# One feed-forward chunk and a copy of the first input chunk at another distance from the weights

## The chip, the cores and the metric

One NeuronCore of a Trainium2 chip runs the whole kernel; the other cores are idle. The metric is the device time of one execution in microseconds (us). TensorE (PE, with its weight loads as PEld), VectorE (DVE), ScalarE (ACT), GpSimd (POOL) and SyncE (SP) each work through a queue of their own, in order, and wait for one another by semaphores.

## The reference: what is computed

Two layers (`DEPTH = 2`) over 256 tokens of width 1024. Each layer is a half-step SwiGLU feed-forward (FFN), a token mixer with three attention branches, and a second feed-forward, each inside a sandwich of RMS norms and with shift, scale and gate from a conditioning vector. The part that the change touches:

```
def swiglu(h, w_gate, w_up, w_down):
    return (jax.nn.silu(h @ w_gate) * (h @ w_up)) @ w_down

for l in range(DEPTH):
    h = modulate(x, norm_pre[l, 0], ...);  x = residual_add(x, swiglu(h, ...), ...)
    h = modulate(x, norm_pre[l, 1], ...);  x = residual_add(x, token_mixer(h, ...), ...)
    h = modulate(x, norm_pre[l, 2], ...);  x = residual_add(x, swiglu(h, ...), ...)
```

`w_gate` and `w_up` are 1024 x 2816, `w_down` is 2816 x 1024, so there are four feed-forwards in a run. They are called FFN0 to FFN3 here, in order of time: FFN0 and FFN1 are those of layer 0, FFN2 and FFN3 those of layer 1.

## The kernel before, in words

Activations lie transposed in SBUF: 128 partitions are 128 of the features, and 256 columns are the tokens. Every fp32 operand of a product is split into a high part of type `float32r` and a low remainder, and a product is three matmuls (`mm3`, L172 to L174): high weights by high activations, high weights by low activations, low weights by high activations. The weights are the loaded (stationary) operand, 128 x 128, and the activations stream past them, 128 x 256. `lin` runs `mm3` over the 128-row chunks k of the contraction into one PSUM tile, so a gate or up tile takes 8 x 3 = 24 matmuls, and a down tile 22 x 3 = 66. Each matmul comes with a weight load of its own.

The modulated input of a feed-forward is `hT[0][k]` and `hT[1][k]` (tiles `h0`, `h1`, high and low, k = 0 to 7; `hact(i, k)` picks one). The inner activation is `mid[0][n]` and `mid[1][n]`, n = 0 to 21, each a tile of 256 columns or 1024 bytes per partition. Weights arrive by SP's DMA queue as `raw`, ACT casts them to `whi` (L166) and DVE subtracts to `wlo` (L167), six buffers each. Small pads (`gap`, 64 bytes or some more) stand between the allocations. By the allocation of the built program every chunk of `h` and `mid` that is streamed begins at a byte address that is 288 modulo 512, and every 128-column weight tile that is loaded beside it at 352 modulo 512; the distance from weights to activations is thus -64 bytes (modulo 512) for nearly all of the kernel's matmuls.

`ffn` (from L353) has these stages. Three of the four feed-forwards begin with an entry: `enter` starts the first six gate tiles from the raw residual (L279, 258 columns, streamed from the tiles `wd8_*`, whose rows are 1032 bytes apart), then `finish` makes the eight modulated chunks (`pn` on DVE L249, `h0` on ACT L251, `h1` on DVE L252), and PE runs the first three up tiles side by side as the chunks appear. FFN0 begins with `opening` instead, which does eight gate and eight up tiles chunk by chunk as the weights arrive. Then comes the loop over `todo`, one `lin` per gate or up tile: 28 tiles in FFN0 and 38 in each other one (the first three of the 38 are those that run side by side). `evac` empties a tile: a SiLU on ACT for gate tiles, and for up tiles a product on DVE (`m`, L379), a cast on ACT to `mid[0][n]` (L383) and a subtraction on DVE to `mid[1][n]` (L384). The last stage is the down projection: four groups of two output tiles, chunk 0 to 21, 132 matmuls each.

The order on each engine is set by the tile framework: it takes the instructions in program order, except that those under `high_priority` come earlier and those under `issue_after` behind a named one, and it estimates when an engine is free. So a new instruction can move others beside it.

Of the kernel before, what the change touches and what calls it, by code (L numbers as in the profile page):

```python
# [11 lines left out]
F32 = mybir.dt.float32  # L12
F32R = mybir.dt.float32r
# [6 lines left out]
S = 256  # L20
DFF = 2816
KC = D // 128
EPS = 1e-6
NEG = -1e30
NO = 8
GATED = 0.65


@with_exitstack
def trunk(ctx, tc, x, c, vecs, ada_w, w_gate, w_up, w_down, w_in, w_uq, w_ukv, w_branch, w_out, rope, out):  # L30
    nc = tc.nc
# [76 lines left out]
    for i in range(0, D, 512):  # L108
        p = ps(512)
# [66 lines left out]
    def lin(o, w, wk, cols, act, ak, nk, start, stop):  # L176

        for k in range(nk):
            mm3(o, w(0, wk + k, cols), w(1, wk + k, cols), act(0, ak + k), act(1, ak + k),
                start and k == 0, stop and k == nk - 1)  # L180
# [45 lines left out]
    def gap(pool, nbytes, name):  # L226
        pool.tile([128, nbytes // 4], F32, name=name)
# [123 lines left out]
    NF = DFF // 128  # L351

    def ffn(l, f, s, opening=None, ahead=None):  # L353
        with ExitStack() as es:
            midp = es.enter_context(tc.tile_pool(name="mid", bufs=1))
            ftmp = es.enter_context(tc.tile_pool(name="ftmp", bufs=2))
            if opening is None:
                wdp = es.enter_context(tc.tile_pool(name="wdp", bufs=1))
                gap(wdp, 64, "gap4")
            mid = [[midp.tile([128, S], F32R, name=f"mid{i}_{n}") for n in range(NF)] for i in range(2)]  # L360
            sg = {}
            last_silu = [None]

# [34 lines left out]
            if opening is None:  # L398
                todo = ([(0, n) for n in range(6)] + [(1, n) for n in range(6)] + todo[12:])
                first = [(ps(S + 2, kind="lin" if i < 2 else "att"),) + weights(*t) for i, t in enumerate(todo[:6])]  # L400
                rp, finish = enter(l, s, first, [wdp.tile([128, FIRST], F32R, name=f"wd8_{i}") for i in range(2)])
                evac(*todo[0], first[0][0], rp)
                finish()
                for i in range(1, 6):
                    evac(*todo[i], first[i][0], rp)
                todo = todo[6:]
            else:
                opening(W, evac)
            for i, (src, n) in enumerate(todo):
                ada_until(l, s, GATED * i / len(todo))  # L410
                p = ps()
                w, cols = weights(src, n)
                lin(p, w, 0, cols, hact, 0, KC, True, True)
                evac(src, n, p)
            table_after(SQRT, last_silu[0])
            if opening is not None:
# [2 lines left out]
            gc = post_col(l, s, 0.5)  # L419
            if opening is not None:  # L420
                wdp = es.enter_context(tc.tile_pool(name="wdp", bufs=1))
                gap(wdp, 64, "gap4")
            for g in range(D // 256):
                pp = [ps(), ps()]
                for k0 in range(0, NF, 8):
# [575 lines left out]
```

## Time and profile before

| | us |
|---|---|
| median of 3 runs | 1311.8 |
| lowest, highest run | 1305.99, 1315.94 |
| the profiled execution, whole | 1306.87 |
| its span, first to last instruction | 1305.0 |
| PE busy in the span | 1279.3 (98%) |
| DVE busy | 990.3 (76%) |
| ACT busy | 758.6 (58%) |

The profile is of one execution. "Busy" for PE counts the time in which at least one matmul is under way; matmuls overlap one another (one lasts 0.28 us, and the next begins about 0.12 us after it), so a busy PE can still be faster or slower. What counts is the time from one matmul's start to the next one's, here called the pitch. Times in the rows are us from the span's start.

### The profile page before, as it was taken

The numbers are of one execution on the slowest core, as the hardware profiler recorded it, in microseconds if no ns is written. First come the engines' busy times: TensorE is split into PE (matmuls) and PEld (weight loads), VectorE is DVE, ScalarE is ACT, GpSimd is POOL, SyncE is SP. The second block draws the span as 40 slices with busy tenths as digits, with TensorE's granted clock in tenths as the row PEclk, the third lists the DMA queues.
The fourth block names the chain that finished last, engine by engine and source line by source line (L and its number), as shares of the span: only waits on it lengthen the run. The fifth ranks groups of instructions, "written<-read, shape, count | busy, mean of one in ns | idle before, by whom it ended". The sixth has DMA issues, their size and how long they took to land.

```text
span 1305.0 us, 26411 instructions
## 1 busy us (share of the span) xinstructions
PE 1279.3 (98%) x10626; PEld 1236.9 (95%) x10626; DVE 990.3 (76%) x1717; ACT 758.6 (58%) x1284; POOL 70.5 (5%) x140
## 2 busy tenths in 40 slices
PE   7999999999999999999999999999999999999997
PEld 6999999998899999999999999999898999999997
DVE  8987777768778798777698777786767969976552
ACT  4655555665865665554565554477577665745551
POOL 0000100000000000001000001000000000000000
PEclk9999999999999999999999999999999999999999
DMA  9988782636567647888928888645467477585550
GB/s 358 364 303 301 272 313 99 195 118 219 199 234 249 213 167 260 268 273 282 322 82 289 277 265 297 243 138 175 149 214 247 163 246 249 155 284 185 177 186 33
DMA packets 82924, 295.73 MB, mean 227 GB/s; under 512 B 9201, under 2 KB 9585, under 8 KB 82802
## 3 DMA queue, kind: packets, MB, share of 16 engines
q1 hardware_dynamic: 64370, 226.94, 50.7%
q0 software_dynamic: 18432, 67.12, 15.8%
q8 instruction: 83, 1.36, 0.4%
q14 instruction: 39, 0.32, 0.1%
HBM read 292.97 MB, written 1.05 MB: 225 GB/s over the span
## 4 chain that ended last, share of the span: by engine, by line
PE 91%; ACT 4%; DVE 3%; issue 1%; DMA 0%; SPq 0%
PE lin L172 25%; PE lin L174 25%; PE lin L173 24%; PE att L279 5%; PE lin L279 3%; PE att L865 1%; PE sum L547 1%; PE lin L865 1%; ACT whi L166 1%; DVE wlo L167 1%; PE att L582 1%; PE att L557 1%; DVE h L252 1%; PE att L611 1%; PE sum L194 1%
## 5 line engine op out<-in xcount | busy, mean ns | idle before, releaser
L167 DVE TENSOR_TENSOR wlo<-raw,whi 128x1024 fp32r<-128x1024 f32 (+2 forms) x382 | 453.0, 1197 | 145.5 <-ACT whi L166 140.2
L172 PE MATMUL lin<-h,whi 128*128 128x256 f32 x1808 | 503.2, 281 | 1.3 <-DVE m L379 1.0
L173 PE MATMUL lin<-h,whi 128*128 128x256 f32 x1808 | 501.7, 279 | 2.2 <-DVE h L252 2.0
L166 ACT CAST whi<-raw 128x1024 fp32r<-128x1024 f32 (+2 forms) x382 | 391.9, 1033 | 189.1 <-PE lin L173 147.3
L174 PE MATMUL lin<-h,wlo 128*128 128x256 f32 x1808 | 501.0, 278 | 0.4 <-DVE wlo L167 0.4
L172 PEld LDWEIGHTS lin<-h,whi 128*128 128x128 f32 x1808 | 338.7, 188 | 5.5 <-ACT h L251 2.6
L173 PEld LDWEIGHTS lin<-h,whi 128*128 128x128 f32 x1808 | 339.7, 188 | 3.8 <-DVE h L252 3.8
L174 PEld LDWEIGHTS lin<-h,wlo 128*128 128x128 f32 x1808 | 338.9, 188 | 0.9 <-DVE wlo L167 0.9
L119 DVE SCALAR_TENSOR_TENSOR ada<-ada,cb 128x1024 f32<-128x1024 f32 x128 | 153.9, 1219 | 25.7 <-DMA ada<-in_ada_w_dram 25.7
L172 PE MATMUL lin<-mid,whi 128*128 128x256 f32 x592 | 164.9, 278 | 0.0
L173 PE MATMUL lin<-mid,whi 128*128 128x256 f32 x592 | 164.9, 278 | 0.0
L174 PE MATMUL lin<-mid,wlo 128*128 128x256 f32 x592 | 164.9, 278 | 0.0
L133 POOL DMA_DIRECT2D ada<-in_ada_w_dram x128 | 67.7, 529 | 1048.1 <-DVE ada L119 1024.5
L173 PEld LDWEIGHTS lin<-mid,whi 128*128 128x128 f32 x592 | 111.8, 189 | 0.0
L172 PEld LDWEIGHTS lin<-mid,whi 128*128 128x128 f32 x592 | 111.8, 189 | 0.0
L174 PEld LDWEIGHTS lin<-mid,wlo 128*128 128x128 f32 x592 | 111.1, 188 | 0.0
L383 ACT CAST mid<-m 128x256 fp32r<-128x256 f32 x88 | 35.1, 407 | 74.6 <-DVE m L379 74.6
L172 PE MATMUL lin<-ybhi,whi 128*128 128x256 f32 x192 | 54.3, 283 | 2.0 <-DVE gb L536 2.0
L173 PE MATMUL lin<-yblo,whi 128*128 128x256 f32 x192 | 53.6, 279 | 0.0
L174 PE MATMUL lin<-ybhi,wlo 128*128 128x256 f32 x192 | 53.6, 279 | 0.0
L384 DVE TENSOR_TENSOR mid<-m,mid 128x256 fp32r<-128x256 f32 x88 | 36.5, 421 | 14.7 <-ACT mid L383 14.7
L370 ACT ACTIVATE sg<-lin 128x256 f32<-128x256 f32 x65 | 24.5, 380 | 31.2 <-PE lin L174 31.2
(288 smaller groups left out, 1912.8 us busy)
## 6 DMA issues: line engine op xcount, KB each, us to landing
ada<-in_ada_w_dram POOLq DMA_DIRECT2D x128, 512.0 KB, 5.0
raw<-in_mix_w_in_dram SPq DMA_DIRECT2D x100, 512.0 KB, 5.1
raw<-in_ffn_w_gate_dram SPq DMA_DIRECT2D x88, 512.0 KB, 5.1
raw<-in_ffn_w_up_dram SPq DMA_DIRECT2D x88, 512.0 KB, 5.4
raw<-in_ffn_w_down_dram SPq DMA_DIRECT2D x80, 512.0 KB, 4.8
raw<-in_mix_w_branch_dram SPq DMA_DIRECT2D x24, 512.0 KB, 5.6
oada<-in_ada_w_dram SPq DMA_DIRECT2D x16, 512.0 KB, 7.3
raw<-in_mix_w_out_dram SPq DMA_DIRECT2D x16, 512.0 KB, 5.3
```

The costliest lines, as they stand in the source:

```text
L119: return nc.vector.scalar_tensor_tensor(raw, raw, 1.0, cb, op0=OP.mult, op1=OP.mult, accum_out=modc[:, l, i, k:k + 1])
L133: nc.gpsimd.dma_start(raw, ada_w[al, i * D + k * 128:i * D + k * 128 + 128, :])
L166: nc.scalar.copy(hi, raw)
L167: nc.vector.tensor_sub(lo, raw, hi.bitcast(F32))
L172: nc.tensor.matmul(o, whi, ahi, start=start, stop=False)
L173: nc.tensor.matmul(o, whi, alo, start=False, stop=False)
L174: nc.tensor.matmul(o, wlo, ahi, start=False, stop=stop)
L279: done.append(nc.tensor.matmul(p[:, cols_of], w(i, k, cols), act[j][:, cols_of], start=start and i == j == 0, stop=stop and j == 1, skip_g ...
L370: last_silu[0] = nc.scalar.activation(sg[n], p[:, :S], AF.Silu)
L383: nc.scalar.copy(mid[0][n], m)
L384: anchor[:] = [nc.vector.tensor_sub(mid[1][n], m, mid[0][n].bitcast(F32))]
L865: nc.tensor.matmul(banks[j][:, a * 256:(a + 1) * 256], parts[k][a][i == 1][:, j * 128:(j + 1) * 128], hact(i == 2, k), start=(k == 0 and a ...
```

## The change

Three things change, all in `ffn`. The tiles of the last inner chunk, `mid[0][21]` and `mid[1][21]`, become longer (by 128 and by 16 columns), and the chunk is a view that begins 126 and 14 columns, that is 504 and 56 bytes, into its tile. The pad `gap4` (64 bytes) goes away, so that what follows lies 576 - 64 = 512 bytes further on than before. And a copy of the first modulated chunk, `hT[i][0]`, is made in that view by one cast on ACT and one on DVE; the tiles at positions 2, 4 and 9 of `todo` stream the copy as their chunk k = 0. The view is overwritten with the inner chunk 21 later. The values that are computed are the same.

```
--- before.py
+++ after.py
@@ -23,6 +23,7 @@
 NO = 8
+TURNS = (2, 4, 9)
 GATED = 0.65
@@ -356,8 +357,13 @@
             if opening is None:
                 wdp = es.enter_context(tc.tile_pool(name="wdp", bufs=1))
-                gap(wdp, 64, "gap4")
-            mid = [[midp.tile([128, S], F32R, name=f"mid{i}_{n}") for n in range(NF)] for i in range(2)]
+            mid = [[midp.tile([128, S + (0 if n < NF - 1 else (128, 16)[i])], F32R, name=f"mid{i}_{n}")
+                    for n in range(NF)] for i in range(2)]
+
+
+            for i, at in enumerate((126, 14)):
+                mid[i][-1] = mid[i][-1][:, at:at + S]
+            turned = lambda i, k: mid[i][-1] if k == 0 else hT[i][k]
             sg = {}
             last_silu = [None]
@@ -406,11 +412,13 @@
                 todo = todo[6:]
             else:
                 opening(W, evac)
+            nc.scalar.copy(mid[0][-1], hT[0][0].bitcast(F32))
+            nc.vector.tensor_copy(mid[1][-1], hT[1][0].bitcast(F32))
             for i, (src, n) in enumerate(todo):
                 ada_until(l, s, GATED * i / len(todo))
                 p = ps()
                 w, cols = weights(src, n)
-                lin(p, w, 0, cols, hact, 0, KC, True, True)
+                lin(p, w, 0, cols, turned if i in TURNS else hact, 0, KC, True, True)
                 evac(src, n, p)
             table_after(SQRT, last_silu[0])
             if opening is not None:
@@ -419,7 +427,6 @@
             gc = post_col(l, s, 0.5)
             if opening is not None:
                 wdp = es.enter_context(tc.tile_pool(name="wdp", bufs=1))
-                gap(wdp, 64, "gap4")
```

By the allocation of the built program only chunk 21 changes its address modulo 512: its high part begins at 280 (-72 bytes from the weights, was -64) and its low part at 344 (-8 bytes from the weights, was -64). All else that a matmul reads keeps its distance. The instructions that stream the shifted view are 3 x 3 in each gate and up stage and 8 x 3 in each down projection, 33 per feed-forward and 132 in all.

The first place is PE's queue in FFN0, at the third tile of `todo`. In the names, `lin_889` or `lin_891` is the tile before it, `h0`, `h1` are the modulated chunks and `mid0_21`, `mid1_21` the shifted view. Before:

```order
L173 MATMUL lin_889<-h1_139,whi_859 128x256
L174 MATMUL lin_889<-h0_138,wlo_860 128x256
L172 MATMUL lin_920<-h0_138,whi_923 128x256
L173 MATMUL lin_920<-h1_139,whi_923 128x256
L174 MATMUL lin_920<-h0_138,wlo_924 128x256
L172 MATMUL lin_920<-h0_138,whi_923 128x256
```

After the change, at the same place:

```order
L174 MATMUL lin_891<-h1_139,whi_861 128x256
L175 MATMUL lin_891<-h0_138,wlo_862 128x256
L173 MATMUL lin_922<-mid0_21_172,whi_925 128x256
L174 MATMUL lin_922<-mid1_21_194,whi_925 128x256
L175 MATMUL lin_922<-mid0_21_172,wlo_926 128x256
L173 MATMUL lin_922<-h0_138,whi_925 128x256
```

The order and the number of matmuls stay; three of them read the copy.

The second place is DVE's queue at the entry of FFN1, where PE waits for the chunks `h1` (L252, L253 after the change) that DVE makes, and for `m` behind them. Before:

```order
L328 TENSOR_SCALAR shift<-att 128x1 x2
L167 TENSOR_TENSOR wlo<-raw,whi 128x1024
L252 SCALAR_TENSOR_TENSOR h_139<-pn,modc,h_138 128x256 x2
L249 SCALAR_TENSOR_TENSOR pn<-xT,acol,sum 128x256 x2
L167 TENSOR_TENSOR wlo<-raw,whi 128x1024
L252 SCALAR_TENSOR_TENSOR h_139<-pn,modc,h_138 128x256
L167 TENSOR_TENSOR wlo<-raw,whi 128x1024
L252 SCALAR_TENSOR_TENSOR h_139<-pn,modc,h_138 128x256
L167 TENSOR_TENSOR wlo<-raw,whi 128x1024
L379 TENSOR_TENSOR m<-lin,yT 128x256 x2
```

After the change:

```order
L329 TENSOR_SCALAR shift<-att 128x1 x2
L416 CAST mid_21_5918<-h_139 128x256
L253 SCALAR_TENSOR_TENSOR h_139<-pn,modc,h_138 128x256 x2
L250 SCALAR_TENSOR_TENSOR pn<-xT,acol,sum 128x256 x2
L168 TENSOR_TENSOR wlo<-raw,whi 128x1024
L253 SCALAR_TENSOR_TENSOR h_139<-pn,modc,h_138 128x256 x2
L168 TENSOR_TENSOR wlo<-raw,whi 128x1024
L385 TENSOR_TENSOR m<-lin,yT 128x256 x2
```

The new cast stands ahead of the chunks, and two of the four `wlo` subtractions have moved from ahead of `m` to behind it. FFN3 changes in the same way; in FFN2 the cast is added and nothing else moves. On ACT the cast to `mid0_21` stands behind the second `h0` chunk, ahead of a `whi` cast and of the SiLU table load, in all three. In FFN0 both casts stand inside `opening`. The order of POOL and SP does not change.

## Rows read from the trace of the kernel before

**Rows 1.** The page: busy time of PE and DVE, granted clock in 40 slices.

```profile
PE 1279.3 (98%) x10626; PEld 1236.9 (95%) x10626; DVE 990.3 (76%) x1717; ACT 758.6 (58%) x1284; POOL 70.5 (5%) x140
PEclk9999999999999999999999999999999999999999
```

**Rows 2.** The page: the chain that ended last, by engine and line.

```profile
PE 91%; ACT 4%; DVE 3%; issue 1%; DMA 0%; SPq 0%
```

**Rows 3.** PE by stretch: stretch, us, busy (matmuls), granted clock, DMA share, GB/s.

```profile
62.00:140.00 78.00, 78.00 (x665) 1.00 0.87 299
141.00:200.00 59.00, 59.00 (x503) 1.00 0.86 304
497.00:591.00 94.00, 94.00 (x832) 1.00 0.81 275
592.00:649.00 57.00, 57.00 (x505) 1.00 0.90 309
684.00:783.00 99.00, 99.00 (x875) 1.00 0.84 277
784.00:838.00 54.00, 54.00 (x479) 1.00 0.91 313
1135.00:1231.00 96.00, 96.00 (x817) 1.00 0.70 224
1232.00:1292.00 60.00, 60.00 (x512) 1.00 0.38 121
```

**Rows 4.** Groups of PE by line: 62 to 140 us (first), 497 to 591 us (second).

```profile
L172 PE MATMUL lin<-h,whi 128*128 128x256 f32 x221 | 62.1, 281 | 0.0
L172 PE MATMUL lin<-h,whi 128*128 128x256 f32 x277 | 76.5, 276 | 0.0
```

**Rows 5.** PE in order of time, FFN2's `enter`: first matmuls of chunks k = 0 to 3.

```profile
655.59 0.40 PE L279 MATMUL lin<-wd,whi 128*128 128x256 f32 x2
...
657.75 0.28 PE L279 MATMUL lin<-wd,whi 128*128 128x258 f32 x1
...
659.89 0.28 PE L279 MATMUL lin<-wd,whi 128*128 128x258 f32 x1
...
662.02 0.28 PE L279 MATMUL lin<-wd,whi 128*128 128x258 f32 x1
```

**Rows 6.** PE in order of time: the mixer's first tile behind `enter`.

```profile
224.97 0.28 PE L172 MATMUL lin<-h,whi 128*128 128x256 f32 x1
...
225.67 0.28 PE L172 MATMUL lin<-h,whi 128*128 128x256 f32 x1
```

**Rows 7.** PE by stretch in the mixer of layer 0.

```profile
235.00:242.00 7.00, 7.00 (x64) 1.00 0.82 267
307.00:318.00 11.00, 11.00 (x97) 1.00 0.73 247
331.00:338.00 7.00, 7.00 (x64) 1.00 0.39 140
447.00:459.00 12.00, 12.00 (x104) 1.00 0.95 319
```

**Rows 8.** DVE in order of time, entry of FFN1; the last row, FFN2.

```profile
489.10 1.22 DVE L167 TENSOR_TENSOR wlo<-raw,whi 128x1024 fp32r<-128x1024 f32 x1
490.23 0.88 DVE L252 SCALAR_TENSOR_TENSOR h<-pn,modc,h 128x256 fp32r<-128x256 f32 x2
...
496.00 0.42 DVE L379 TENSOR_TENSOR m<-lin,yT 128x256 f32<-128x256 f32 x1
...
675.76 0.88 DVE L252 SCALAR_TENSOR_TENSOR h<-pn,modc,h 128x256 fp32r<-128x256 f32 x2 [0.46 <-ACT h L251]
```

**Rows 9.** PE in order of time: first matmul on `h`, then that of the fourth tile (FFN1, FFN2).

```profile
484.90 0.28 PE L172 MATMUL lin<-h,whi 128*128 128x256 f32 x1
...
496.48 0.38 PE L172 MATMUL lin<-h,whi 128*128 128x256 f32 x1 [0.50 <-DVE m L379]
...
673.68 0.28 PE L172 MATMUL lin<-h,whi 128*128 128x256 f32 x1
...
684.13 0.38 PE L172 MATMUL lin<-h,whi 128*128 128x256 f32 x1
```

**Rows 10.** The page: groups of 128x256 casts and subtractions into `mid`.

```profile
L383 ACT CAST mid<-m 128x256 fp32r<-128x256 f32 x88 | 35.1, 407 | 74.6 <-DVE m L379 74.6
L384 DVE TENSOR_TENSOR mid<-m,mid 128x256 fp32r<-128x256 f32 x88 | 36.5, 421 | 14.7 <-ACT mid L383 14.7
```

More of the change, by code (lines that the diff above doesn't have):

```diff
@@ L25 @@
 NO = 8
+TURNS = (2, 4, 9)
 GATED = 0.65
@@ L358, in ffn @@
                 wdp = es.enter_context(tc.tile_pool(name="wdp", bufs=1))
-                gap(wdp, 64, "gap4")
-            mid = [[midp.tile([128, S], F32R, name=f"mid{i}_{n}") for n in range(NF)] for i in range(2)]
+            mid = [[midp.tile([128, S + (0 if n < NF - 1 else (128, 16)[i])], F32R, name=f"mid{i}_{n}")
+                    for n in range(NF)] for i in range(2)]
+            for i, at in enumerate((126, 14)):
+                mid[i][-1] = mid[i][-1][:, at:at + S]
+            turned = lambda i, k: mid[i][-1] if k == 0 else hT[i][k]
             sg = {}
@@ L408, in ffn @@
                 opening(W, evac)
+            nc.scalar.copy(mid[0][-1], hT[0][0].bitcast(F32))
+            nc.vector.tensor_copy(mid[1][-1], hT[1][0].bitcast(F32))
             for i, (src, n) in enumerate(todo):
@@ L412, in ffn @@
                 w, cols = weights(src, n)
-                lin(p, w, 0, cols, hact, 0, KC, True, True)
+                lin(p, w, 0, cols, turned if i in TURNS else hact, 0, KC, True, True)
                 evac(src, n, p)
@@ L421, in ffn @@
                 wdp = es.enter_context(tc.tile_pool(name="wdp", bufs=1))
-                gap(wdp, 64, "gap4")
             for g in range(D // 256):
```

## The prediction

> **What bounds the kernel.** Read the page's busy times first: PE has a matmul under way in 98% of the span, at a granted clock of nine tenths or more in every slice, which is the higher level of 2.4 GHz [rows 1]. The chain of work that ended last says the same: 91% of it is PE [rows 2]. So time can only come from fewer matmuls, from shorter waits at the few places where PE has any, or from a smaller pitch, the time from one matmul's start to the next. The first is not touched here.
>
> For the pitch, read PE by stretch in the four feed-forwards [rows 3]. A stretch counts every matmul that overlaps it, and one lasts 0.28 us, so the pitch is (length + 0.28) / count. FFN0 gives 78.28 / 665 = 0.1177 us in its gate and up stage and 59.28 / 503 = 0.1179 in its down projection. FFN1 gives 0.1133 and 0.1134, FFN2 0.1135 and 0.1133, FFN3 0.1178 and 0.1177. The clock is 1.00 in all eight, PE is never idle in them, and the shapes are the same. The groups by line show it as a duration: the same matmul takes 281 ns in FFN0 and 276 ns in FFN1 [rows 4]. So there are two pitches, 117.7 and 113.3 ns, each held through a whole feed-forward, gate stage and down projection alike, and nothing in the instructions picks between them. The mixer shows both as well: 7.28 / 64 = 0.1138 in two stretches, 11.28 / 97 = 0.1163 and 12.28 / 104 = 0.1181 in two others [rows 7], with restarts of PE between them. I read this as two ways in which the stream of activations and the stream of weight loads can lie against each other in time, each of which keeps itself up until something disturbs it.
>
> Does the distance in SBUF matter to this? One stretch says so. In `enter`, chunk k = 0 is streamed from `wd8`, 256 columns, at distance 0 from the weights where all else has -64 bytes (the addresses are those of the built program), and its 18 matmuls take 657.75 - 655.59 = 2.16 us: 120.0 ns each, neither of the two pitches [rows 5]. The next two chunks lie 8 and 16 bytes further off; their 18 matmuls of 258 columns take 2.14 and 2.13 us, 118.9 and 118.3 ns.
>
> **The change, part by part.**
>
> *The turned matmuls* are 33 per feed-forward. What one costs itself at the distances -72 and -8 no row shows. The floor is the smaller pitch, no cost; the nearest row is the stretch at distance 0, 120.0 ns. I take that: 132 x (120.0 - 113.3) = 0.9 us, range 0 to 0.9.
>
> *What they do to the pitch behind them* is the main term, and I assume that a few matmuls at another distance shift the two streams until they fall into the smaller pitch, and that this pitch survives the next such matmuls. Then FFN0 and FFN3 gain 117.7 - 113.3 = 4.4 ns per matmul. FFN0 has 28 x 24 + 4 x 132 = 1200 steady matmuls: 5.3 us. FFN3 has 35 x 24 + 528 = 1368: 6.0 us. FFN1 and FFN2 have the smaller pitch already in this execution and gain nothing. Together 11.3 us. Before the first turn the old pitch lasts two tiles in FFN0 (48 x 4.4 ns = 0.2) and about one in FFN3 (0.1): 0.3 us back.
>
> *The casts at the entries.* There PE waits for DVE: from its first matmul on `h` to that of the fourth tile 496.48 - 484.90 = 11.58 us pass in FFN1, with the last wait on `m` [rows 9], where 72 matmuls at 113.3 ns would need 8.2. DVE runs without a gap from 489.10 to `m` at 496.00 [rows 8], so what stands in its queue there is on the path. A cast like the new one takes 0.42 us on DVE and 0.41 on ACT [rows 10]. But in FFN1 and FFN3 the order also moves two `wlo` subtractions from ahead of `m` to behind it, and each takes 490.23 - 489.10 = 1.13 us of DVE's queue [rows 8]. FFN2, which has one `wlo` fewer there already, needs 684.13 - 673.68 = 10.45 us [rows 9], 1.13 less than FFN1: a `wlo` taken out of the way has come back in full. So FFN1 and FFN3 could each gain 2 x 1.13 - 0.42 = 1.8 us. Against it, DVE waits 0.46 us for ACT's `h0` at the entry of FFN2 [rows 8], and ACT gets the same cast there; and the two subtractions have to be done a little later, beside tiles that PE runs without waiting in FFN2, whose order is already this one. I take 1.5 us each, and 0.4 lost in FFN2: a gain of 2.6, range from a loss of 1.2 (three casts, nothing back) to a gain of 3.2. In FFN0 the two casts stand in `opening`, where DVE is the busy engine: a loss of 0.4 at most, which I take.
>
> *The shift of what lies behind `mid`* is 512 bytes, and the distances stay as they were: nothing. The casts to chunk 21 now write to the shifted view, 407 and 421 ns each [rows 10], with a whole tile's time on PE (24 x 0.113 = 2.7 us) to hide them: nothing. Were that cover gone, four times 0.8 us would show.
>
> **The sum** is made against the profiled execution's own 1306.9 us: 1306.9 - 11.3 + 0.3 + 0.9 - 2.6 + 0.4 = 1294.6, say 1295. The median of the runs is 1311.8, 4.9 more than the profiled one, and the highest is 9.0 more. One more feed-forward at the larger pitch would be 1368 x 4.4 ns = 6.0 us, so I take the runs to differ in how many of the four fall into it. If the turns work, this spread goes too, and the gain against the median is larger, 1.3%.
>
> **The rivals.**
>
> *Re-drawn.* A disturbance might settle the pitch either way, like the restarts in the mixer, two of which end at each pitch among the four shown [rows 7]. Then half of all matmuls in the feed-forwards are at the larger one. All four slow would cost 5.3 + 3 x 6.0 = 23.3 us over all fast; half of that, 11.7, is what this execution has now. With the other terms (0.9 - 2.6 + 0.4 = -1.3) the time is 1306 us, 6 to either side for one feed-forward. For it: nothing in the rows says that one pitch is sturdier than the other. Against: there are eleven turns in a feed-forward, and if the smaller pitch is kept even a little more often than the larger one, it wins.
>
> *Nothing happens.* The two pitches might come from something that addresses do not touch, the moment at which PE starts behind a wait. Then all stays as it falls out, with the entries' gain: 1306.9 - 2.2 = 1305 up to 1311.8 - 2.2 = 1310 with the median's luck. For it: a pitch outlasts thousands of changes of tile. Against it: the 120.0 ns at distance 0 [rows 5]. The Trainium skill speaks for this rival: its page SBUF — State Buffer (section SBUF: two separate sides) says that among the engine ports only the pair that VectorE and GpSimd share causes contention and that PE never waits on anyone. The trace does not bear this out as it stands: equal matmuls at an equal clock take 113.3, 117.7 and, at distance 0, 120.0 ns, with PE waiting for no engine.
>
> *The turn leaves the larger pitch.* This is the rival on the other side, and a row speaks for it: `enter` ends on matmuls at a distance that isn't the usual one, and the six matmuls on `h` right behind it in the mixer of layer 0 take 225.67 - 224.97 = 0.70 us, 117 ns each [rows 6]. If a turn does that every time, FFN1 and FFN2 lose 2 x 6.0 = 12.0 us and FFN0 and FFN3 gain nothing: 1306.9 + 12.0 - 1.3 = 1317.6. It decides from the point where FFN1 and FFN2 lose more matmuls to the larger pitch than FFN0 and FFN3 gain at the smaller; 1311.8 is passed where the balance is one feed-forward. Against it: that stretch has 258 columns and runs through all distances from 0 to 56 bytes, where a turn is three matmuls of 256.
>
> **How the numbers follow.** The forecast gets 0.55, re-drawn 0.2, nothing 0.1, left at the larger pitch 0.15. The forecast's own range is 1291 (the entries give all, the turned matmuls cost nothing) to 1301 (the entries give nothing back, and a tenth to a quarter of the matmuls stay at the larger pitch). The range that should hold 8 times in 10 goes from there up to the re-drawn and the unchanged case, 1312, and leaves out the last rival and the tails. About 1% is what a measurement of this kernel can tell from no change: below 1298.7 is faster, above 1324.9 slower. The forecast lies below 1298.7 in some eight of ten of its cases, 0.44, and the re-drawn case adds 0.03; above 1324.9 only the far end of the last rival lies, 0.03. The rest is within 1%.
>
> **What would show it.** In the profile after, FFN0 and FFN3 by stretch should count as FFN1 and FFN2 do now: 94 us should hold about 832 matmuls, and `L173` on `h` (L172 before) should take 276 ns. The pitch should change at a turned tile, not at a wait. The entry of FFN1 and FFN3 should last some 10 us instead of 11.58, that of FFN2 10.8. I am wrong if the large pitch stands behind turned tiles, if the pitch changes in the middle of a down projection behind chunk 21, or if PE gets new waits for `wlo` behind the entries.

## The result, and the profile after

| | before | after |
|---|---|---|
| median of 10 runs each | 1306.16 us | 1295.32 us |
| lowest and highest | 1300.85, 1315.94 | 1293.13, 1301.27 |
| ratio after / before | | 0.9911, 95% interval 0.9888 to 0.9934 |
| profiled execution: its time, its span | 1306.87, 1305.0 us | 1295.14, 1293.2 us |

The kernel got 0.9% faster, and the predicted 1295.0 us lies 0.3 us below the median. The median of before that stood beside the prediction, 1311.8 us, came from three runs; ten runs put it at 1306.16, so the gain is 0.9% and not the 1.3% that the prediction gave against the median.

The page of the kernel after, the rows that answer to [rows 1]: PE has 13.1 us less busy time with the same number of matmuls, at the same granted clock.

```profile
PE 1266.2 (98%) x10626; PEld 1225.1 (95%) x10626; DVE 990.6 (77%) x1721; ACT 759.4 (59%) x1288; POOL 70.8 (5%) x140
PEclk9999999999999999999999999999999999999999
```

PE by stretch in the kernel after, the answer to [rows 3] (stretch, us, busy and matmuls, granted clock, DMA share, GB/s): gate stage and down projection of FFN0, FFN1, FFN2 and FFN3 in turn.

```profile
74.00:134.00 60.00, 60.00 (x531) 1.00 0.90 305
144.00:194.00 50.00, 50.00 (x442) 1.00 0.91 313
497.00:590.00 93.00, 93.00 (x822) 1.00 0.84 283
592.00:642.00 50.00, 50.00 (x442) 1.00 0.88 310
684.00:783.00 99.00, 99.00 (x876) 1.00 0.84 281
784.00:832.00 48.00, 48.00 (x424) 1.00 0.91 312
1133.00:1225.00 92.00, 92.00 (x814) 1.00 0.71 237
1226.00:1274.00 48.00, 48.00 (x424) 1.00 0.45 142
```

With the formula of the prediction the gate stages have (60.28 / 531) 113.5, 113.5, 113.3 and 113.4 ns per matmul; FFN0 and FFN3 had 117.7 and 117.8 [rows 3]. The down projections have 50.28 / 442 = 113.8 and 48.28 / 424 = 113.9 ns, half a nanosecond more than the 113.3 to 113.4 of FFN1 and FFN2 before.

Groups of PE by line between 74 and 134 us in the kernel after: the matmul on `h` takes 276 ns where it took 281 [rows 4].

```profile
L173 PE MATMUL lin<-h,whi 128*128 128x256 f32 x176 | 48.6, 276 | 0.0
```

The pitch changes at the first turned tile. PE in order of time in FFN0 after: the head of the tile before it, that of the turned tile and its sixth matmul, and the head of the next.

```profile
65.12 0.28 PE L173 MATMUL lin<-h,whi 128*128 128x256 f32 x1
...
67.95 0.28 PE L173 MATMUL lin<-mid,whi 128*128 128x256 f32 x1
...
68.55 0.28 PE L175 MATMUL lin<-h,wlo 128*128 128x256 f32 x1
...
70.70 0.28 PE L173 MATMUL lin<-h,whi 128*128 128x256 f32 x1
```

The tile before takes 2.83 us, 24 x 117.9 ns, and the turned one 2.75. Within the turned tile the three turned matmuls and the two behind them are 120 ns apart ((68.55 - 67.95) / 5), and from the sixth on it is 113 ((70.70 - 68.55) / 19).

In FFN1 and FFN3 the same can be read behind the entry. PE in order of time, kernel after: in FFN1 the head of the first tile that PE runs by itself (position 3, not turned), of the turned tile at position 4 and of the next one; then the first two of these in FFN3.

```profile
491.02 0.28 PE L173 MATMUL lin<-h,whi 128*128 128x256 f32 x1
...
493.85 0.28 PE L173 MATMUL lin<-mid,whi 128*128 128x256 f32 x1
...
496.61 0.28 PE L173 MATMUL lin<-h,whi 128*128 128x256 f32 x1
...
1127.10 0.28 PE L173 MATMUL lin<-h,whi 128*128 128x256 f32 x1
...
1129.82 0.28 PE L173 MATMUL lin<-mid,whi 128*128 128x256 f32 x1
```

FFN1 comes out of its entry at the large pitch (2.83 us for 24 matmuls, 117.8 ns), and the tile at position 4 turns it. FFN3 comes out at the small one (2.72 us, 113.3 ns) before that tile, so in this execution there was nothing to turn in FFN3.

By stage, worked out from the starts of the matmuls in the two traces (us, after minus before):

| stage | FFN0 | FFN1 | FFN2 | FFN3 |
|---|---|---|---|---|
| opening or entry, and gate stage | -1.90 | -1.23 | +0.56 | -5.10 |
| down projection | -1.97 | +0.27 | +0.27 | -2.04 |

The mixers give -0.14 and -0.32, the four `enter` stages nothing. Against before, FFN0 and FFN3 have the pitch's gain, FFN1 and FFN3 a shorter entry, FFN2 a longer one, and every down projection that was already at the small pitch pays 0.27 us.

### The profile page after: what moved, and what is told of

It reads as the page before. It is cut to its first block, busy times and chain, and to the rows that moved or that the text cites. A ratio compares the mean times of both kernels' runs of the same rounds, so it can differ in the third digit from the quotient of the medians.

```text
span 1293.2 us, 26410 instructions
## 1 busy us (share of the span) xinstructions
PE 1266.2 (98%) x10626; PEld 1225.1 (95%) x10626; DVE 990.6 (77%) x1721; ACT 759.4 (59%) x1288; POOL 70.8 (5%) x140
## 5 line engine op out<-in xcount | busy, mean ns | idle before, releaser
L173 PE MATMUL lin<-h,whi 128*128 128x256 f32 (+1 forms) x1796 | 497.2, 279 | 2.9 <-ACT h L252 2.9
L174 PE MATMUL lin<-h,whi 128*128 128x256 f32 (+1 forms) x1796 | 495.6, 277 | 0.2
L175 PE MATMUL lin<-h,wlo 128*128 128x256 f32 (+1 forms) x1796 | 495.0, 277 | 0.4 <-DVE wlo L168 0.4
L173 PEld LDWEIGHTS lin<-h,whi 128*128 128x128 f32 (+1 forms) x1796 | 335.4, 188 | 6.3 <-ACT h L252 4.9
L174 PEld LDWEIGHTS lin<-h,whi 128*128 128x128 f32 (+1 forms) x1796 | 336.6, 188 | 1.1 <-DVE h L253 1.1
L175 PEld LDWEIGHTS lin<-h,wlo 128*128 128x128 f32 (+1 forms) x1796 | 336.5, 188 | 0.9 <-DVE wlo L168 0.9
L173 PE MATMUL lin<-mid,whi 128*128 128x256 f32 x604 | 167.2, 277 | 0.0
L174 PE MATMUL lin<-mid,whi 128*128 128x256 f32 x604 | 167.1, 277 | 0.0
L174 PEld LDWEIGHTS lin<-mid,whi 128*128 128x128 f32 x604 | 113.5, 188 | 0.0
L173 PEld LDWEIGHTS lin<-mid,whi 128*128 128x128 f32 x604 | 113.4, 188 | 0.0
```

Source lines behind the costliest of these rows:

```text
L173: nc.tensor.matmul(o, whi, ahi, start=start, stop=False)
L174: nc.tensor.matmul(o, whi, alo, start=False, stop=False)
L175: nc.tensor.matmul(o, wlo, ahi, start=False, stop=stop)
```

## The experiments

The edits are against the kernel after. Two readings of it had to be told apart first: that the address of the chunk does it, or that something else in the change does (the copy, the casts and the order that they bring). Then which distances do it, what a turn costs, and where the entries' gain comes from.

### The usual distance

```
-            for i, at in enumerate((126, 14)):
+            for i, at in enumerate((0, 0)):
```

The order of all instructions, the copies and the casts stay; chunk and copy lie at -64 bytes like all else.

> The same program as the changed kernel, instruction for instruction, but the last inner chunk and the copy begin at the start of their tiles, so they lie at -64 bytes from the weights like everything else. Theory D (distance): three matmuls at the usual distance disturb nothing. FFN0 runs at 117.7 ns a matmul from beginning to end (in the changed kernel only for the first two tiles of its loop), so FFN0's loop and down projection together take about 4.5 to 5 us more than in the changed kernel; FFN1 to FFN3 keep whatever pitch they enter with, without a change of pitch at a turned tile or behind chunk 21. Median 1299 to 1313 us, moving with the number of slow feed-forwards, ratio to the kernel before 0.995 to 1.0 (the entries' 2 us stay). Theory C (the copies and the other order at the entries did it, the address nothing): the same as the changed kernel, about 1295 us, ratio about 0.991, FFN0 at 113.3 ns.

Measured: 1304.60 us median of 10, before 1305.31; ratio 0.9993, 0.9964 to 1.0022. PE by stretch in this kernel, gate stages of FFN0, FFN1, FFN2 and FFN3:

```profile
68.00:136.00 68.00, 68.00 (x580) 1.00 0.86 290
497.00:590.00 93.00, 93.00 (x792) 1.00 0.82 276
684.00:782.00 98.00, 97.91 (x859) 1.00 0.82 271
1145.00:1230.00 85.00, 85.00 (x752) 1.00 0.73 239
```

FFN0 and FFN1 are at 117.7 and 117.8 ns, FFN2 at 114.3 (its stretch begins inside the entry, with the waits there; from the entry on it is 113.3) and FFN3 at 113.4. The order of the instructions on PE, VectorE, ScalarE and GpSimd is that of the kernel after, one for one, so the address is what matters. And the slow pair is another one than before: it was FFN0 and FFN3 [rows 3]. With all distances alike the pitch of FFN1, FFN2 and FFN3 falls out anew behind each entry, and it is kept to the end of the down projection; FFN0 began its gate stage at the large pitch in all fourteen traces of this study. The 60 runs of before that stood beside the kernels of this study say the same: 17 of them lie between 1298.9 and 1301.4 us, 18 between 1305.3 and 1307, and 8 between 1311.5 and 1313.6, some 6 us apart, which is what one feed-forward makes.

### Either part alone

```
-            for i, at in enumerate((126, 14)):
+            for i, at in enumerate((126, 0)):
```

> Only the high part of the chunk and of the copy is shifted (-72 bytes from the weights), the low part lies at the usual -64. Theory D1 (any of the shifted matmuls is enough): as in the changed kernel, 113.3 ns within some five matmuls behind every turned tile, FFN0 to FFN3 all at 113.3 ns, span about 1293 us. Theory D2 (the low part, 56 bytes away from its usual place, does it): the pitch does not change at the turns, FFN0 stays at 117.7 ns, span 1297 to 1310 us.

and the other way round, `(0, 14)`:

> Only the low part is shifted (-8 bytes from the weights), the high part lies at the usual -64. Theory D1 (any of the shifted matmuls is enough): 113.3 ns behind every turn, span about 1293 us. Theory D3 (the high part, which two of the three matmuls stream, does it): no change of pitch at the turns, FFN0 at 117.7 ns, span 1297 to 1310 us.

Measured, one run each: 1296.55 us with the high part at -72 alone, 1304.93 with the low part at -8 alone. Gate stages of FFN0 and FFN3 by stretch, first the high part alone, then the low part alone:

```profile
68.00:136.00 68.00, 68.00 (x601) 1.00 0.87 299
1145.00:1230.00 85.00, 85.00 (x752) 1.00 0.68 224
```

```profile
68.00:136.00 68.00, 68.00 (x580) 1.00 0.86 294
1145.00:1230.00 85.00, 85.00 (x724) 1.00 0.69 225
```

The high part at -72 does it alone. The low part at -8 turns nothing: FFN0 and FFN3 stay at 117.7 ns through eleven turned tiles each, and FFN1 and FFN2, which were drawn small, stay small (823 matmuls in 93 us).

### Distance zero

```
-            for i, at in enumerate((126, 14)):
+            for i, at in enumerate((16, 16)):
```

> Both parts lie at the weights' own address modulo 512 (distance 0, where a long stretch of the kernel before ran at 120.0 ns). Theory E (any other distance disturbs and the engine then falls into the small pitch): all four feed-forwards at 113.3 ns behind their turns, span about 1293 us. Theory F (the distance decides where it falls): at distance 0 the engine comes back at 117.7 ns, also from the small pitch, so the feed-forwards run at 117.7 ns behind turns, span 1310 to 1318 us, FFN1 and FFN2 included.

Measured: 1294.51 us in one run. All four feed-forwards go to the small pitch, FFN0 with 602 matmuls in the 68 us that held 601 above. The stretch at distance 0 in `enter` [rows 5] is slower while it lasts, and yet a turn at 0 leaves the small pitch behind it here. Further down one such turn fails.

### Where the turns stand

Chunk 21 back at the usual distance, only the copy turned:

```
-            for i, at in enumerate((126, 14)):
-                mid[i][-1] = mid[i][-1][:, at:at + S]
-            turned = lambda i, k: mid[i][-1] if k == 0 else hT[i][k]
+            copies = [mid[i][-1][:, at:at + S] for i, at in enumerate((126, 14))]
+            for i in range(2):
+                mid[i][-1] = mid[i][-1][:, :S]
+            turned = lambda i, k: copies[i] if k == 0 else hT[i][k]
...
```

> Theory G: a turn costs about 34 ns (a turned down projection took 60.89 us where an unturned one at the small pitch took 60.62, eight turns), and nothing but the first turn is needed, since the small pitch keeps itself up. With chunk 21 back at the usual distance and only the copy still turned, each of the four down projections loses 0.27 us, 1.1 in all: 1294.2 us against 1295.3 of the changed kernel, and all four hold the small pitch to their end (60.6 us each, FFN3's 62.1). Rival H: the turns in the down projection are what holds the small pitch there. Then one or more down projections fall back to the large pitch somewhere, 528 x 4.4 ns = 2.3 us each, and the time is 1296.5 us or more.

The other half: no copy, no casts, chunk 21 at -72 and -8. The order of PE, VectorE and ScalarE is then that of the kernel before.

```
-            nc.scalar.copy(mid[0][-1], hT[0][0].bitcast(F32))
-            nc.vector.tensor_copy(mid[1][-1], hT[1][0].bitcast(F32))
...
-                lin(p, w, 0, cols, turned if i in TURNS else hact, 0, KC, True, True)
+                lin(p, w, 0, cols, hact, 0, KC, True, True)
```

> No copy of chunk 0, no cast at the entries, the order of PE, VectorE and ScalarE as in the kernel before; chunk 21 lies at -72 and -8 bytes, so the first turn comes in the down projection. Theory G with the order as the cause of the shorter entries: the entries go back to 11.58, 10.45 and 11.57 us (2.3 us more than the changed kernel in sum), and the gate stages have the pitch that the restart gives them: if FFN0 and FFN3 are the slow ones, as before, 672 x 4.4 + 840 x 4.4 ns = 6.7 us. The down projections go to the small pitch at the first chunk 21, 22 tiles-parts in. Time 1295.3 + 2.3 + 6.7 - 0.4 (twelve gate turns fewer) + 1.0 (the beginnings of two down projections) = 1305 us, and 1298 to 1302 if fewer gate stages are slow. Rival: the entries stay at 10.2 us (then it was the pitch, not the order, that shortened them), and the time is 2.3 us lower, or the down projection of FFN0 stays at the large pitch behind chunk 21.

and the kernel after as it is, beside them:

> The changed kernel as it is, on the same chip as the three others: 1295.3 us, ratio to the kernel before 0.991.

Measured: the turned gate alone 1294.11 us (6 runs, 1293.18 to 1296.96), the turned down projections alone 1300.30 (10 runs, 1298.47 to 1308.82), the kernel after 1294.45 (6 runs, 1294.16 to 1295.47). Between the first and the last the times cannot tell, the traces can: without turns the down projections take 60.62, 60.62, 60.60 and 62.07 us, with them 60.88 to 60.90 three times and 62.38, so they cost 0.26 to 0.31 each, 1.1 in all, and hold nothing: the small pitch goes through without them.

The second kernel isolates the entries. Rows of PE at its entry of FFN1 and FFN3: the first matmul on `h` and that of the fourth tile, in brackets what PE waited for.

```profile
483.24 0.28 PE L173 MATMUL lin<-h,whi 128*128 128x256 f32 x1
...
494.80 0.39 PE L173 MATMUL lin<-h,whi 128*128 128x256 f32 x1 [0.52 <-DVE m L385]
...
1123.89 0.28 PE L173 MATMUL lin<-h,whi 128*128 128x256 f32 x1
...
1135.46 0.39 PE L173 MATMUL lin<-h,whi 128*128 128x256 f32 x1 [0.50 <-DVE m L385]
```

That is 11.56 and 11.57 us, the 11.58 of before [rows 9], with the wait on `m`. In the kernel after the same distance is shorter, and the wait is gone (PE, FFN1, then FFN2):

```profile
480.76 0.28 PE L173 MATMUL lin<-h,whi 128*128 128x256 f32 x1
...
491.02 0.28 PE L173 MATMUL lin<-h,whi 128*128 128x256 f32 x1
...
668.58 0.28 PE L173 MATMUL lin<-h,whi 128*128 128x256 f32 x1
...
679.51 0.39 PE L173 MATMUL lin<-h,whi 128*128 128x256 f32 x1
```

10.26 and 10.93 us; FFN3 has 10.22. The kernel at the usual distance, which has the casts and the new order but no turn, has 10.27, 10.92 and 10.22. So the order that the casts bring is the whole of the entries' gain, and the pitch has no part in it: entry and gate stage of FFN1 and FFN3 take 106.88 and 106.89 us with the old order and 105.50 and 105.64 with the new one (the turned gate alone), all four at the small pitch. VectorE's queue in the kernel after shows why, as [rows 8] did for before: `m` has two `wlo` fewer ahead of it.

```profile
484.94 0.28 DVE L416 CAST mid<-h 128x256 fp32r<-128x256 f32 x1
...
489.13 1.22 DVE L168 TENSOR_TENSOR wlo<-raw,whi 128x1024 fp32r<-128x1024 f32 x1
490.26 0.75 DVE L385 TENSOR_TENSOR m<-lin,yT 128x256 f32<-128x256 f32 x2
490.93 1.22 DVE L168 TENSOR_TENSOR wlo<-raw,whi 128x1024 fp32r<-128x1024 f32 x1
```

What else this kernel loses are the gate stages that are drawn large, FFN0 and FFN2 in the profiled execution (1303.53 us), whose down projections come to the small pitch right behind the first chunk 21. The expected 1305 us supposed two such stages; the median of 1300.3 suggests that in most runs there are fewer.

### Twelve turns in each mixer

The mixer shows both pitches too [rows 7], so a turn there might pay: a copy of the high part of chunk 2 at distance 0, read in the first tile of twelve bursts of projections and once in the output projection; in the feed-forwards the copy at distance 0 in two tiles, and chunk 21 unturned.

```
+            hx = mp.tile([128, S], F32R, name="hx")
...
+            def bent(i, k):
+                return hx if i == 0 and k == 2 else hT[i][k]
...
+            nc.scalar.copy(hx, hT[0][2].bitcast(F32))
...
```

> Built to beat the changed kernel: turns at distance 0 in two tiles of each gate stage, none in the down projections, and in each mixer a copy of the high part of chunk 2 at distance 0, used in the first tile of each of twelve bursts of projections and once in the output projection. Theory G: 1.1 us from the down projections, and in each mixer about 270 of the 330 slow matmuls in bursts and 90 of the slow ones in the output projection turn fast, 360 x 4.4 ns = 1.6 us, less 13 turns x 0.03 = 0.4: 1.2 us each. 1295.3 - 1.1 - 2.4 = 1291.8 us. Rival J: the restart behind each burst decides the pitch and a high part alone at distance 0 doesn't turn it: the mixers stay as long as they were, 1294.2 us, or 1294.9 with the turns' cost.

Measured: 1294.06 us (12 runs, 1291.71 to 1304.48). In the profiled execution, one of the slower ones (1299.11), the mixers take 238.21 and 237.61 us, no less than 237.61 and 237.79 in the kernel after on the same chip, and FFN1 is at the large pitch from end to end (its down projection takes 62.86 us) although two of its tiles are turned. Its gate stage by stretch:

```profile
497.00:590.00 93.00, 93.00 (x792) 1.00 0.82 274
```

So a turn at distance 0 can miss. In the mixers it misses too, at one and the same of the twelve places in both. The seven tiles at the start of the second branch gate do turn small in both mixers (168 x 4.4 ns = 0.7 us); why the mixers are no shorter for it, whether by the cost of the turns in bursts that were small anyway or by how the other bursts fell out, was not followed up. The expected 1291.8 us was missed by 2.3. Which bursts are large without turns, the other traces tell: in nine traces without turns in the mixer, so in 18 mixers, ten tiles of projections are at the large pitch every time (seven at the start of the second branch gate and three in the middle of the third), and most others never.

### One distance after the other

If -72 always turns, -8 of the low part never, and 0 mostly, is it the distance, or the part? In two kernels one copy, of the high or of the low part alone, is rewritten at another offset after each turned tile, so that every second tile of a gate stage has another distance. Chunk 21 is unturned, so that each pitch lasts until the next turned tile.

```
...
+            view = lambda j: room[0][:, CHAIN[j][1]:CHAIN[j][1] + S]
...
+            turned = lambda j: lambda i, k: view(j) if k == 0 and i == CHAIN[j][0] else hT[i][k]
...
-                lin(p, w, 0, cols, turned if i in TURNS else hact, 0, KC, True, True)
+                lin(p, w, 0, cols, turned(i // 2 - 2) if i % 2 == 0 and 4 <= i < 4 + 2 * len(CHAIN) else hact, 0, KC, True, True)
...
```

> One copy at a time of chunk 0, always of the high or of the low part alone, rewritten on ScalarE at another offset after each turned tile, so that every second tile of the gate stage from the fifth on is turned by another distance, in this order: low part -72; high part -8, -56, -48, -32, -16, 0, +64, +192, -192, -128, -72 bytes modulo 512. Chunk 21 of the down projection is at the usual distance. FFN0 has started at the large pitch in every trace so far, so its pitch shows the first distance that turns. Theory L (the role: a turn works when two of three matmuls are moved): the low part at -72 leaves FFN0 at 117.7 ns, the high part at -8 two tiles later brings it to 113.3. Theory M (the distance): the low part at -72 brings it to 113.3 at once. If neither does, -8 is inert in either part and the first of the others shows where it begins. Behind the flip each tile shows what a turn of that distance costs from the small pitch: 20 to 45 ns in tiles of 24 matmuls. Time 1294 to 1297 us.

> The same with other distances: high part +192, +64, -192, +128, +256, -128, -96 bytes modulo 512, then the low part at +192, 0, -128, then the high part at 0 and -32. Theory L: the first turned tile, the high part at +192, brings FFN0 from 117.7 to 113.3 ns, as any shifted high part does. Rival N (only small distances around zero turn, -72 and 0 as seen): +192, -192, +128 and +256 leave it at 117.7 ns and cost nothing. Time 1294 to 1300 us.

Measured: 1299.12 and 1311.00 us, one run each and both longer than expected. PE in order of time in FFN0 of the first kernel: the first turned matmul of the first seven turned tiles, at low -72, then high -8, -56, -48, -32, -16 and 0. From one to the next are 48 matmuls (47 from the first): 5.44 us at the small pitch, 5.65 at the large one.

```profile
75.00 0.28 PE L175 MATMUL lin<-mid,whi 128*128 128x256 f32 x1
...
80.33 0.28 PE L174 MATMUL lin<-mid,whi 128*128 128x256 f32 x1
...
85.98 0.28 PE L174 MATMUL lin<-mid,whi 128*128 128x256 f32 x1
...
91.46 0.28 PE L174 MATMUL lin<-mid,whi 128*128 128x256 f32 x1
...
96.92 0.28 PE L174 MATMUL lin<-mid,whi 128*128 128x256 f32 x1
...
102.58 0.28 PE L174 MATMUL lin<-mid,whi 128*128 128x256 f32 x1
...
108.06 0.28 PE L174 MATMUL lin<-mid,whi 128*128 128x256 f32 x1
```

The low part at -72 brings FFN0 from the large to the small pitch with a single matmul (5.33 us for 47), so at -72 either part turns and it needs no two matmuls. The high part at -8 puts it back to the large one (5.65), -56 to the small one (5.48), -32 to the large one again (5.66), -16 to the small one (5.48), and from there on it stays. Here the part does count: the low part at -8 had left FFN1 and FFN2 at the small pitch. FFN1, FFN2 and FFN3 repeat this tile by tile, with both falls at the same two distances.

The second kernel, FFN0, heads of the turned tiles at high +192 and +64, and further down at high 0 and -32, the last row being the start of the down projection:

```profile
73.45 0.28 PE L174 MATMUL lin<-mid,whi 128*128 128x256 f32 x1
...
79.11 0.28 PE L174 MATMUL lin<-mid,whi 128*128 128x256 f32 x1
...
84.58 0.28 PE L174 MATMUL lin<-mid,whi 128*128 128x256 f32 x1
...
128.29 0.28 PE L174 MATMUL lin<-mid,whi 128*128 128x256 f32 x1
...
133.76 0.28 PE L174 MATMUL lin<-mid,whi 128*128 128x256 f32 x1
...
139.41 0.28 PE L174 MATMUL lin<-mid,whi 128*128 128x256 f32 x1
```

+192 does not change the large pitch (5.66), +64 ends it (5.47), and -32, the last turn of every gate stage here, brings it back (5.65 after 5.47). All four down projections then stay at the large pitch, 62.89, 62.89, 62.87 and 64.42 us, where the first kernel has 60.63, 60.63, 60.60 and 62.07. This is the rival that ends on the other side: a turn at the wrong distance in the last place costs 9.1 us in the down projections and, by 38 gate tiles at the large pitch from it on, 38 x 24 x 4.4 ns = 4.0 us before them; the one run lies 4 us above the median of before beside it, 1306.99. (Some 3 us of that are not the turns: its second mixer and the `enter` behind it are 1 to 2 us longer each than in the other traces, which was not followed up.)

What the traces show, by distance of the streamed chunk from the weights:

| part and distance | met at the large pitch | met at the small pitch |
|---|---|---|
| high -72 (low at -64 or -8) | small each time, in 15 feed-forwards of seven kernels | stays small |
| low -72 | small (1 of 1) | stays small |
| high -56, -16 | small (4 of 4 each) | not seen |
| high +64 | small (1 of 1) | stays small |
| both at 0 | small in 6 of 7 feed-forwards | stays small |
| high 0 | in both mixers small at the second branch gate, missed at one place | stays small |
| high +192, low -8 | stays large | stays small |
| high -8 | not seen | **large (4 of 4)** |
| high -32 | not seen | **large (8 of 8)** |
| high -192, -128, -96, -48, +128, +256; low 0, -128, +192 | not seen | stays small |

What a tile with one of these turns takes above 24 x 113.3 ns, met at the small pitch, goes by the distance too: nothing at +192, 14 ns at +64 and -192, some 27 at 0, 48 at -72 of the high part alone.

In all these kernels the weights stay at 352 and the other chunks at 288 modulo 512. So the distance from the weights, the chunk's own address and its distance from the chunks before and behind it change together, and which of them counts is not shown; nor is it that 512 is the right period, since no distance was tried a second time 512 bytes further on.

### A version built to beat both

Turns only where they pay: the copy at -72 and -8 in the same three tiles of each gate stage, no turned chunk 21, and in each mixer a high part at -72 in four tiles, three of them at the head of the bursts that are always drawn large, and once in the output projection.

```
+            hx = mp.tile([128, S + 112], F32R, name="hx")[:, 110:110 + S]
...
+                starts = {1: (0, 4), 0: (5,), 2: (3,)}[n]
...
-                    lin(p, ws[m // 2], 0, cols[m % 2], hact, 0, KC, True, True)
+                    lin(p, ws[m // 2], 0, cols[m % 2], bent if m in starts else hact, 0, KC, True, True)
```

> The changed kernel with chunk 21 back at the usual distance, the copy turned in the same three tiles of each gate stage, and in each mixer a high part of chunk 2 at -72, used in four tiles that head a burst (in the branch gates, where the traces so far show the large pitch in 18 of 18 mixers for three of the four) and once in the output projection. Theory G: 1.1 us from the down projections; in each mixer 10 tiles that were always at the large pitch, 240 x 4.4 ns = 1.1 us, about half of 72 and of 192 other matmuls, 0.6 us, less 5 x 0.04 = 0.2: 1.5 us each. 1295 - 1.1 - 3.0 = 1291 us. Rival: as with twelve turns a mixer at distance 0, which gave 0.3 us each, the turns cost what they give: 1294 us.

beside the kernel after once more:

> The changed kernel as it is, on the same chip as the kernel with chosen turns: 1295 us.

Measured: 1292.79 us (6 runs, 1290.75 to 1296.82), between the two times expected; the kernel after 1296.43 (5 runs, 1295.13 to 1297.82), before 1306.99 (12 runs); the ratios to before are 0.9888 (0.9849 to 0.9927) and 0.9912 (0.987 to 0.9955). The intervals overlap, so the times alone don't settle it; the traces say where 5.1 us of span went (1289.1 against 1294.2): 1.1 in the down projections, and 2.0 and 1.7 in the mixers, 236.68 and 236.70 us against 238.68 and 238.39. No mixer without turns is that short: in the twelve traces of kernels that turn nothing there, the 24 mixers take 237.61 to 240.27 us. The ten tiles that are always large make 240 x 4.4 ns = 1.1 us of it in each; the rest may be how the other bursts fell out in these two executions. PE by stretch at the second branch gate of both mixers, first this kernel, then the kernel after:

```profile
304.00:322.00 18.00, 18.00 (x162) 1.00 0.72 236
947.00:965.00 18.00, 18.00 (x162) 1.00 0.59 208
```

```profile
304.00:322.00 18.00, 18.00 (x157) 1.00 0.69 229
947.00:965.00 18.00, 18.00 (x159) 1.00 0.74 254
```

## Why the prediction was right, and where it was not

*The pitch.* All four feed-forwards run at the small pitch, and where the pitch changes it changes at a turned tile: as forecast. Since the span of the profiled execution of before had just two feed-forwards at the large pitch, the forecast 11.3 - 0.3 = 11.0 us are there: FFN3 alone is 7.14 us shorter; 1.4 of that are its entry, and its turns give back 0.4, which leaves 6.1 for the forecast 5.9. But the feed-forwards that were turned are not those of the forecast. It let FFN1 enter at the small pitch and FFN3 at the large one, as before; in the kernel after it was the other way round, so FFN0 and FFN1 were turned, and FFN3 fell out small by itself. The sum holds because every draw ends at the small pitch: in the six kernels that turn this tile at -72, 7 of 18 feed-forwards came out of their entry large, and all 7 were turned at position 4. The turn at position 2, inside the entry, does not decide it.

*The assumption under it was too wide.* The step said that "a few matmuls at another distance shift the two streams until they fall into the smaller pitch". Other distances do it, or do nothing, or do the opposite. At -72 it holds every time. Had the high part been placed at -8 or -32, the rival *the turn leaves the larger pitch* would have come true, as the four down projections behind -32 show. That -72 is one of the distances that help was luck; the rows before could not tell these apart: the one stretch at another distance [rows 5] showed the pitch during it, and [rows 6], which I held against the forecast with 0.15, was a draw of the restart.

*A turned matmul.* The term took 6.7 ns, the excess of the stretch at distance 0, and no effect on the neighbours: 0.9 us for 132. But the three turned matmuls cost more than that, and the two behind them are late as well: from start to start 119, 125, 122, 124 and 116 ns (tile at position 9 of FFN1). A turned gate tile has 115.0 ns against 113.3, 24 x 1.7 = 41 ns, and a turned tile of the down projection 0.27 / 8 = 34 ns. Eight and three of these make 0.4 us per feed-forward, 1.6 in all, above the range of 0 to 0.9 that the step gave. The nearest row had the price of a steady stretch at another distance, and a turn is two changes of distance; that these are what costs is my reading.

*The entries.* 1.5 us in FFN1 and FFN3 each and -0.4 in FFN2. With the old order and the same pitch the gate stages of FFN1 and FFN3 are 1.38 and 1.25 us longer, with some 0.1 of turns to be added, and FFN2 pays 0.56, of which 0.1 are turns: 1.5, 1.4 and -0.4. A `wlo` that leaves VectorE's queue ahead of `m` comes back nearly in full, as [rows 8, 9] had it. The cast on VectorE was over-priced: it takes 0.28 us, where I took the 0.42 of a subtraction [rows 10].

*The casts in FFN0.* I took 0.4 us at most, and it is 0.8. The first 96 matmuls of `opening` on `h` take 12.44 us in both traces without the casts (before, and the turned down projections alone), and 13.24 to 13.41 us in eleven of the twelve with them (12.76 in the other). PE waits there for the second chunk of `h`; first before, then after:

```profile
22.48 0.97 PE L865 MATMUL lin<-h,whi 128*128 128x256 f32 x6 [0.35 <-ACT h L888]
```

```profile
23.09 0.96 PE L872 MATMUL lin<-h,whi 128*128 128x256 f32 x6 [1.57 <-ACT h L895]
```

ScalarE's cast holds up a `whi`, for which VectorE now waits 0.62 us, and VectorE's own cast puts off what is behind it by 0.21 more: `pn` of that chunk starts 7.99 us behind the first of these matmuls instead of 7.16. How much of this is still there at the end of the stage varies. From PE's first matmul to the end of FFN0's gate stage the six traces with the copy at -72 take 136.24 to 136.86 us, where pitch and turns alone give 138.32 - 2.96 + 0.2 + 0.1 = 135.7.

*The sum* with what was measured: 1306.9 - 11.0 + 1.6 - 2.5 + 0.8 - 0.5 (the mixers) = 1295.3, and the profiled execution took 1295.14. The turns cost 0.7 more than forecast, FFN0's opening 0.4 more, the entries gave 0.1 less, and the mixers gave 0.5 by luck. So the near hit of the time owes 0.5 us to luck; the main term is right by its mechanism.

*The spread.* The prediction laid the runs' spread to the number of slow feed-forwards and expected it to go. It went in part: 1293.13 to 1301.27 against 1300.85 to 1315.94. Part of what is left is the mixers' own draw, which no turn of this change touches: in the three traces of the kernel after both mixers together take 475.4 to 477.1 us. Another part is the granted clock: the two longest of the ten runs, 1299.69 and 1301.27 us, have a mean of 0.995 where the other eight have 0.997 or 0.998, and those eight end at 1296.11. A clock lower by 0.003 would make 3.9 us of such a span, an estimate from these figures. From the three runs I had taken 1311.8 for the usual time; it is one step of 6 us above it, and so the gain read 1.3% and the chance of more than 1% 0.47; it is 0.9%.

*The other rivals.* The time of *re-drawn* is what the kernel at the usual distance shows, 1304.6 us for a forecast 1306, but there the entries draw the pitch and not the turns. *Nothing happens* fell with the same run. The Trainium skill's page SBUF — State Buffer (section SBUF: two separate sides), which the prediction named for this rival, states that PE never waits on anyone there. That rule gives no reason for what the runs show: the same matmuls in the same order take 1304.6 or 1295.3 us by the address of one chunk in 22 and of one copy. How the address acts inside the chip no run here shows; that the two streams keep up an arrangement in time, as I read it, fits with everything above and isn't proven by it.

## What to carry to other kernels

Where PE is never idle, count its matmuls per stretch before looking anywhere else: a stage that holds 4% fewer of the same shape at the same clock has something to give that no wait will show. If one of two values persists over a thousand matmuls and more, one matmul that reads its operand at another address can move all behind it, but which addresses help has to be tried, since the neighbours of a good one can do harm. And of a kernel whose runs lie in steps, three runs are too few for the time before.

## What was not expected of the hardware

- A single matmul at another distance set the pitch of all that followed up to the next turned tile, and three at the head of a tile that of a whole feed-forward: 113.3 or 117.7 ns, 6.0 us for the 1368 matmuls of FFN1 or FFN3.
- Which pitch follows goes by the distance in no simple order: -8 and -32 of the high part leave the large pitch, -16 between them and -56 and -72 beyond them the small one. +192 bytes did nothing at all, 113.3 ns right through the turned tile.
- A turn at -72 and -8 is felt in five matmuls, the three turned ones and two behind: 34 to 41 ns in all.
- Behind a wait of PE the pitch falls out anew, but not everywhere by chance: ten tiles of the mixer were at the large pitch in 18 of 18 mixers, and FFN0's gate stage began at it in 14 of 14 traces.
